# A two-layer hybrid decoder: value blocks side by side, stores on GpSimd's queue, constants and gates at the passage, the last block in three

## The chip, the cores and the metric

The kernel runs on one core of one Trainium2 chip. The metric is the device time of the program in microseconds, the median of several runs. A profile is one execution of the program that the hardware profiler recorded; its times are microseconds from the first instruction's start. The engines are TensorE (PE: matrix products, with its weight loads as PEld), VectorE (DVE), ScalarE (ACT), GpSimd (POOL) and SyncE (SP, which here only issues transfers). Each runs its own queue of instructions in order and waits for the others by semaphores. SBUF is the on-chip memory, PSUM the accumulators that PE writes.

## The reference

The input `x` is 1024 tokens of 1024 features in float32. Two layers with residuals follow, then a final RMS norm. Layer 0 is a gated linear recurrence and layer 1 is forgetting attention, both widened by a SiLU gate:

```python
def fox_mixer(h, w_in, b_f, w_out):            # layer 1, h = rms_norm(x, norm_g[1])
    u = h @ w_in                               # q, k, v, gate: 1024 each; 16 forget logits
    cum = cumsum(log_sigmoid(f_logit + b_f), axis=1)
    logits = q @ k.T / sqrt(64) + cum[query] - cum[key]      # 16 heads of 64
    p = softmax(where(key <= query, logits, -1e30))
    return (p @ v * silu(gate)) @ w_out
...
x = x + lru_mixer(rms_norm(x, norm_g[0]), ...)
x = x + fox_mixer(rms_norm(x, norm_g[1]), ...)
return rms_norm(x, final_g)
```

In layer 0 the mixer is a causal convolution over 4 tokens, two block-diagonal sigmoid gates, a first-order recurrence over the tokens of 1536 channels, and an output product.

## The kernel before, in words

**Products.** PE multiplies float32 numbers as pairs: each operand is split into a rounded high part and the remainder (`to_hi`, line 82, and `to_lo`, line 95), and a product takes three matmuls (high by high, low by high, high by low; lines 121 to 123 for most). Weights come through `split_weights` (line 98): a load into the buffer `wf` by SP, a cast to `wh` by ACT, the remainder `wl` by POOL or DVE. The buffers have rings: three `wf`, four `wh`, four `wl`. All matmuls go through `matmul` and `transpose` (lines 53 and 57), so in the profile they have lines 54 and 58, and one goes by the names of the tiles.

**PSUM.** There are three rings of two tiles: "g" (one bank: projections, products), "S" (two banks: scores, and the transposed probabilities under the name `pt`) and "O" (one bank: weighted values, small things).

**Order.** The code is a trace, and a planner orders each engine's queue after a model of the times. It may put a later instruction forward if an earlier one would wait. An order is forced where the code stands in `tc.issue_after(i)`: the instructions in it that lie on the engine of `i` come behind `i`. `run` (line 783) uses it to lay out the attention by hand: a string says which of three streams takes the next step, "0" the weighing of a head, "1" the scores of the next, "." a filler (projections for later heads, near the end the output product).

**Layer 0** (lines 175 to 462) goes over 12 channel blocks. At its end the passage to layer 1 (lines 437 to 462) adds the last output products to `x`, stores `x` to DRAM (`x1d`), splits it into the operands `hT` of layer 1 and forms its norms (`rms_row`, with the tile `rs` and the row `rsrow`).

**The start of layer 1** (lines 476 to 636). The causal mask and constant rows of the operand tiles `T` (keys) and `U` (queries) are set first, by POOL and DVE. `kq_units` (line 551) projects keys and queries, here the first half of the tokens for the first two heads. `values(0)` (line 502) projects the values of four heads together with the 16 forget logits: eight blocks of 128 tokens, each over eight k of 128 features, tile `vps`, even blocks in "g" and odd ones in "S"; at the end of a block ACT and DVE take it to the split values `v`, and DVE takes the logits to `fz`. `forget` (line 607) transposes four blocks of `fz` (tile `fps`), forms the log-sigmoids and their running sums, and stores them as pairs (`cumd`), from where they are loaded into rows of `T` and `U`. Line 631 calls ten steps of `values(0)`, `forget(0)`, the rest of the values, `forget(1)`; the second token half of `kq_units` follows at line 932.

**Attention**, head by head (line 941). `maxima` (line 655) makes the scores of 128 queries in S, DVE adds the mask and takes the maximum `m`, ACT takes the exponential `p` with its sum. When a head's eight sums are there, they are inverted, transposed (`tr`), copied to `rc`, stored (`recd`, line 697) and loaded again as rows for all 64 features of the head (`recb`, line 701). `scale` (line 707, POOL) multiplies the gate `sg` by these rows; `weigh` (line 712) transposes `p`, splits it and multiplies it by the values into `yo`; `gated` (line 759, POOL) multiplies `yo` by the gate. Up to pair 5 the result is stored (`y1d`) and loaded near the end; pairs 6 and 7 are split in place by `split_y` (line 797), the former at lines 968 and 980. After every fourth head `values(1)` to `values(3)` run without logits (line 974): half the weights are split ahead of the head's last streams, the rest behind, and all blocks lie in "g".

**The output.** `partial` (line 830) multiplies pairs 0 to 5 by the output weights (`wf<-in_wo`), adds the residual that SP loads (`xp<-x1d`, line 838), and stores it back (`x1d<-xp`, line 842). `turned` (line 861) takes blocks of 128 tokens: it transposes the residual, adds the products of pairs 6 and 7 (tile `turn`, halves of 512 features), ACT squares with a sum (line 891), DVE multiplies by the norm's gain (lines 893 and 896). For the second half of the tokens each block ends at once: `root_mean` (line 905), the scaling of both halves (ACT line 897, DVE line 898), two stores.

Of the kernel before, what the change touches and what calls it, by code (L numbers as in the profile page):

```python
# [11 lines left out]
F32 = mybir.dt.float32  # L12
# [5 lines left out]
P = 128  # L18
SEQ = 1024
HALF = 512  # L20
KT = 8
# [17 lines left out]
def trunk(ctx: ExitStack, tc: tile.TileContext, xt, w0, wg, wo0, pc, gn, gf, w1, wv, wf, bf, wo1, out):  # L39
# [431 lines left out]
    with ExitStack() as l1:  # L471
# [16 lines left out]
        for s in range(2):  # L488
            nc.gpsimd.memset(f32(T[s][64:, 1]), 1.0)
# [12 lines left out]
        def values(g):  # L502
# [11 lines left out]
            for st in range(8):  # L514
                if ex and st % 2:
                    pt = ps.tile([P, SEQ], F32, tag="S", name="vps")[:, : 256 + ex]
                else:
                    pt = ps.tile([P, 256 + ex], F32, tag="g", name="vps")
                c = (st % 4) * P
                for k in range(KT):  # L520
                    xh, xl = hT[st // 4][k]
                    wh, wl = parts[k]
                    xh, xl = xh[:, c : c + P], xl[:, c : c + P]
                    matmul(pt, xh, wh, start=k == 0, stop=False)
                    matmul(pt, xl, wh, start=False, stop=False)
                    matmul(pt, xh, wl, start=False, stop=k == KT - 1)
                    if k % 4 == 1:
                        yield
# [22 lines left out]
        def kq_units(pair, parts=((1, (0, 1)), (0, (0, 1)))):  # L551

            for is_k, hs in parts:
# [78 lines left out]
        for _ in range(10):  # L632
            next(first)
        forget(0)
        drain(first)
        forget(1)
# [18 lines left out]
        def maxima(hd, c):  # L655
# [31 lines left out]
            if hd == HEADS - 1 or c == 1:  # L687
# [9 lines left out]
                nc.sync.dma_start(recd[hd, b0:b1], rc[:nb])  # L697
# [3 lines left out]
                nc.sync.dma_start(  # L701
# [128 lines left out]
        def partial(todo):  # L830

            for db, c in todo:
# [28 lines left out]
        def turned(c, q):  # L861
# [11 lines left out]
            for b in range(2):  # L873
                cs = slice(q * 256 + b * P, q * 256 + (b + 1) * P)
                ss = ssq[c][:, 4 * q + 2 * b : 4 * q + 2 * b + 2]
                for h, hs in enumerate(halves):
                    pt = ps.tile([P, HALF], F32, tag="gO"[c * b], name="turn")

                    for i in range(4):
                        x = xs[4 * h + i][:, b * P : (b + 1) * P]  # L880
                        matmul(pt[:, i * P : (i + 1) * P], x, ident, start=i == 0, stop=False, is_transpose=True)
                    for k in range(2):
                        yh, yl = (z[:, cs] for z in y1[c][6 + k])
                        wh, wl = (z[:, k::2] for z in late_w[h])
# [5 lines left out]
                    sq = at.tile([P, HALF], F32, tag="xp", name="sq1", bufs=2)  # L890
                    nc.scalar.activation(sq, pt, AF.Square, accum_out=ss[:, h : h + 1])
                    if c == 0 or h == 0:
                        nc.vector.tensor_tensor(res[b][:, hs], pt, grow[:, hs], ALU.mult)
                        yield
                if c == 1:
                    r = root_mean(ss, lambda: nc.vector.tensor_tensor(res[b][:, hs], pt, grow[:, hs], ALU.mult))
                    nc.scalar.activation(res[b][:, halves[0]], res[b][:, halves[0]], AF.Copy, scale=r)
# [43 lines left out]
        for hd in range(HEADS):  # L941
# [25 lines left out]
            if hd == 14:  # L967
                split_y(1, 6, yos[6, 1])
# [10 lines left out]
            if hd == 13:  # L979
                split_y(0, 6, yos[6, 0])  # L980
# [90 lines left out]
```

## Time and profile before

| | us |
|---|---|
| three runs | 1137.04, 1137.51 (median), 1138.75 |
| the profiled execution, its own time | 1138.24 |
| its span, first to last instruction | 1136.5 |
| PE busy | 1116.5 |
| DVE, ACT, POOL busy | 757.9, 592.1, 163.5 |
| granted PE clock, mean | 0.999 of full |

How to read the lines below: a row of the order of time has the start, the duration, the engine, the line, the operation, output<-inputs, their shapes, the number of instructions that the row merges, and in brackets how long the engine stood idle before and for whom. A matmul's duration overlaps the next one's start, so its pace is read from starts. A row of the waits reads: who <- for whom: total us, times, longest. A row of the chain has start, length, what; it is the chain of work that ended last, followed back. In the page, x is the number of instructions. A row of SPq is SP's queue, with issues of transfers.

### The profile page before, as it was taken

The numbers are of one execution on the slowest core, as the hardware profiler recorded it, in microseconds if no ns is written. First come the engines' busy times: TensorE is split into PE (matmuls) and PEld (weight loads), VectorE is DVE, ScalarE is ACT, GpSimd is POOL, SyncE is SP. The second block draws the span as 40 slices with busy tenths as digits, with TensorE's granted clock in tenths as the row PEclk, the third lists the DMA queues.
The fourth block names the chain that finished last, engine by engine and source line by source line (L and its number), as shares of the span: only waits on it lengthen the run. The fifth ranks groups of instructions, "written<-read, shape, count | busy, mean of one in ns | idle before, by whom it ended". The sixth has DMA issues, their size and how long they took to land.

```text
span 1136.5 us, 15822 instructions
## 1 busy us (share of the span) xinstructions
PE 1116.5 (98%) x5713; PEld 937.5 (82%) x5713; DVE 757.9 (67%) x1276; ACT 592.1 (52%) x1081; POOL 163.5 (14%) x105
## 2 busy tenths in 40 slices
PE   8999999999999999999999999999999999999997
PEld 7787888888888887888888888888888888878886
DVE  7589756876568689666676466764666645676645
ACT  8388345354453666365555355553555534554435
POOL 1212112121121201420010100101001010010110
PEclk9999999999999999999999999999999999999999
DMA  6111121111202114433525215242142431665445
GB/s 215 52 42 51 42 61 38 52 51 42 61 28 61 51 53 147 130 108 95 121 71 117 71 59 123 80 108 79 58 116 78 114 86 47 180 176 164 155 145 185
DMA packets 63702, 105.43 MB, mean 93 GB/s; under 512 B 9508, under 2 KB 24484, under 8 KB 63624
## 3 DMA queue, kind: packets, MB, share of 16 engines
q1 hardware_dynamic: 63624, 104.42, 31.8%
q8 instruction: 45, 0.74, 0.3%
q14 instruction: 33, 0.27, 0.1%
HBM read 63.30 MB, written 15.93 MB: 70 GB/s over the span
## 4 chain that ended last, share of the span: by engine, by line
PE 89%; DVE 3%; ACT 2%; issue 2%; DMA 2%; POOL 1%; SPq 0%; POOLq 0%; ACTq 0%; DVEq 0%
PE gps L54 33%; PE ops L54 15%; PE ups L54 11%; PE vps L54 7%; PE S L54 6%; PE O L54 6%; PE pt L58 5%; PE turn L54 3%; PE gate L54 2%; DVE sq L162 1%; POOL wl L96 1%; DMA x<-in_xt 1%; DVE wl L96 0%; DVE x L453 0%; DMA wf<-in_wo 0%
## 5 line engine op out<-in xcount | busy, mean ns | idle before, releaser
L54 PE MATMUL gps<-hh,wh 128*128 128x512 f32 x576 | 228.9, 398 | 0.0
L54 PE MATMUL gps<-hl,wh 128*128 128x512 f32 x576 | 226.7, 394 | 0.0
L54 PE MATMUL gps<-hh,wl 128*128 128x512 f32 x576 | 226.6, 393 | 0.0
L85 ACT CAST wh<-wf 128x512 fp32r<-128x512 f32 (+2 forms) x156 | 94.3, 607 | 144.2 <-PE gps L54 47.2
L683 ACT ACTIVATE p<-S,m 128x128 f32<-128x128 f32 (+7 forms) x128 | 94.9, 741 | 135.5 <-DVE m L678 134.4
L96 POOL TENSOR_TENSOR wl<-wf,wh 128x512 fp32r<-128x512 f32 (+1 forms) x60 | 98.1, 1639 | 395.9 <-ACT wh L85 342.8
L96 DVE TENSOR_TENSOR pl<-pt,ph 128x512 fp32r<-128x512 f32 (+1 forms) x198 | 98.6, 540 | 81.3 <-ACT ph L85 81.0
L54 PEld LDWEIGHTS gps<-hl,wh 128*128 128x128 f32 x576 | 108.2, 188 | 24.5
L54 PEld LDWEIGHTS gps<-hh,wl 128*128 128x128 f32 x576 | 108.6, 189 | 19.8
L54 PEld LDWEIGHTS gps<-hh,wh 128*128 128x128 f32 x576 | 108.5, 188 | 19.8
L678 DVE CUSTOM_DVE_ANT_0 S<-S,mask 128x128 f32<-128x128 f32 (+7 forms) x128 | 97.3, 760 | 30.5 <-PE S L54 28.9
L710 POOL TENSOR_TENSOR sg<-sg,recb 64x1024 f32<-64x1024 f32 (+1 forms) x17 | 39.2, 2306 | 460.2 <-DMA recb<-recd 444.6
L85 ACT CAST ph<-pt 128x512 fp32r<-128x512 f32 (+1 forms) x198 | 83.6, 473 | 30.6 <-PE pt L58 25.3
L54 PE MATMUL S<-T,U 96*128 96x512 f32 (+7 forms) x384 | 92.2, 349 | 2.0 <-ACT p L683 2.0
L96 DVE TENSOR_TENSOR wl<-wf,wh 128x512 fp32r<-128x512 f32 x96 | 72.1, 756 | 26.0 <-ACT wh L85 25.3
L361 DVE TENSOR_TENSOR x<-x,ops 128x512 f32<-128x512 f32 x80 | 54.0, 681 | 50.6 <-PE ops L54 50.6
L54 PEld LDWEIGHTS S<-T,U 128*128 128x128 f32 (+1 forms) x384 | 68.7, 190 | 15.9 <-ACT p L683 3.2
L54 PE MATMUL ups<-hh,wh 128*128 128x512 f32 x192 | 75.9, 395 | 4.3 <-ACT hh L87 2.4
L58 PE MATMUL pt<-ident,p 128*128 128x128 f32 x576 | 79.3, 273 | 0.0
L58 PEld LDWEIGHTS pt<-ident,p 128*128 128x128 f32 x576 | 67.4, 140 | 12.4 <-issue 2.2
L54 PE MATMUL vps<-wh,hh 128*128 128x256 f32 (+1 forms) x256 | 73.7, 288 | 3.0 <-DVE sg L649 2.1
L54 PE MATMUL ops<-yh,wh 128*128 128x512 f32 x192 | 76.1, 396 | 0.5 <-DVE x L453 0.5
(176 smaller groups left out, 2259.0 us busy)
## 6 DMA issues: line engine op xcount, KB each, us to landing
wf<-in_w SPq DMA_DIRECT2D x100, 256.0 KB
wf<-in_wo SPq DMA_DIRECT2D x64, 128.0 KB
U<-qkh SPq DMA_DIRECT2D x64, 128.0 KB
T<-qkh SPq DMA_DIRECT2D x28, 256.0 KB
x<-in_xt SPq DMA_DIRECT2D x16, 256.0 KB
x1d<-x SPq DMA_DIRECT2D x16, 256.0 KB
wf<-in_wv SPq DMA_DIRECT2D x16, 256.0 KB
U<-qkl SPq DMA_DIRECT2D x32, 128.0 KB
```

Of the source, the lines that this page charges most:

```text
L54: pe[0] = nc.tensor.matmul(*args, **kw)
L58: pe[0] = nc.tensor.transpose(*args)
L85: nc.scalar.copy(hi, src)
L96: return eng.tensor_tensor(lo, src, f32(hi), ALU.subtract)
L162: eng.tensor_tensor(parts[0], parts[0], sq, ALU.add)
L361: nc.vector.tensor_tensor(x, x, pt, ALU.add)
L678: nc.vector.tensor_tensor_reduce(S[:, :n], S[:, :n], mask[:, SEQ - n :], -1.0, -NEG, ALU.add, ALU.min, accum_out=m)
L683: seen[0] = nc.scalar.activation(p, S[:, :n], AF.Exp, bias=m, scale=-1.0, accum_out=sums[:, i : i + 1])
L710: nc.gpsimd.tensor_tensor(sg, sg, recs[hd // 2][rows, cs], ALU.mult)
```

## The change

Six things change.

- **Values.** In the groups without logits, blocks 0 and 1 run side by side: k 0 to 3 of block 0, k 0 to 3 of block 1, k 4 to 7 of block 0, k 4 to 7 of block 1. Odd blocks lie in "S" in all groups.
- **Constants.** The constant rows and the mask are set after the first two steps of `values(0)`, which hold the split of all its weights.
- **Forget gates.** The transposes are ordered behind PE's last traced matmul. `forget(1)` moves behind all values and lies between the second token half's projections: two transposes, two filler steps (twelve matmuls), the third, two more steps, the fourth and the rest. For the first two heads the casts of that half go from DVE to ACT.
- **Queues.** The store of the sums, the load of their rows and the store of the output sums are issued by POOL instead of SP.
- **Splits.** The two `split_y` of pair 6 have their ACT cast ordered behind the last exponential traced.
- **Last block.** The last 128 tokens of all go in parts of 512, 256 and 256 features, the third in a "g" tile; their sums of squares are added in two steps. The last `run` has 20 steps in place of 18.

```diff
-        mask = tu.tile([P, SEQ], BF16, name="mask")
-        nc.gpsimd.memset(mask, 0.0)
-        nc.gpsimd.affine_select(
-            out=mask, in_=mask, pattern=[[-1, SEQ]], compare_op=ALU.is_ge, fill=NEG, base=SEQ - P, channel_multiplier=1
-        )
...
-        for s in range(2):
-            nc.gpsimd.memset(f32(T[s][64:, 1]), 1.0)
-            for u in U[s][s:]:
-                nc.vector.memset(f32(u[64:, 1]), 0.0)
-                nc.vector.memset(f32(u[64:68, 1]), -1.0)
+        def fixed_rows():
+            for s in range(2):
+                nc.gpsimd.memset(f32(T[s][64:, 1]), 1.0)
+                for u in U[s][s:]:
+                    nc.vector.memset(f32(u[64:, 1]), 0.0)
+                    nc.vector.memset(f32(u[64:68, 1]), -1.0)
...
-            for st in range(8):
-                if ex and st % 2:
+            todo = [(st, k) for st in range(8) for k in range(KT)]
+            if not ex:
+                todo[: 2 * KT] = [(st, k) for h in range(2) for st in range(2) for k in range(h * 4, h * 4 + 4)]
+            pts = {}
+            for st, k in todo:
+                if k == 0:
+                    if st % 2:
                         pt = ps.tile([P, SEQ], F32, tag="S", name="vps")[:, : 256 + ex]
                     else:
                         pt = ps.tile([P, 256 + ex], F32, tag="g", name="vps")
+                    pts[st] = pt
+                pt = pts[st]
...
+                if k < KT - 1:
+                    continue
...
-                eng = nc.vector if pair == 0 else nc.scalar
                 def use(h, pt):
+                    eng = nc.scalar if pair or h else nc.vector
...
             for i in range(4):
-                transpose(pt[:HEADS, i * P : (i + 1) * P], fz[:, half * 4 + i], ident)
+                if half and i > 1:
+                    yield
+                with tc.issue_after(pe[0].ins):
+                    transpose(pt[:HEADS, i * P : (i + 1) * P], fz[:, half * 4 + i], ident)
...
         first = values(0)
-        for _ in range(10):
-            next(first)
-        forget(0)
+        next(first)
+        next(first)
+        fixed_rows()
+        mask = tu.tile([P, SEQ], BF16, name="mask")
+        nc.gpsimd.memset(mask, 0.0)
+        nc.gpsimd.affine_select(
+            out=mask, in_=mask, pattern=[[-1, SEQ]], compare_op=ALU.is_ge, fill=NEG, base=SEQ - P, channel_multiplier=1
+        )
+        take(first, 8)
+        drain(forget(0))
         drain(first)
-        forget(1)
...
-                nc.sync.dma_start(recd[hd, b0:b1], rc[:nb])
+                nc.gpsimd.dma_start(recd[hd, b0:b1], rc[:nb])
...
-                nc.sync.dma_start(
+                nc.gpsimd.dma_start(
                     recs[pair][rows, b0 * P : b1 * P],
...
-                nc.sync.dma_start(x1d[c, :, db], x)
+                nc.gpsimd.dma_start(x1d[c, :, db], x)
-        ssq = [const.tile([P, 8], F32, name=f"ssq{c}") for c in range(2)]
+        ssq = [const.tile([P, 8 + c], F32, name=f"ssq{c}") for c in range(2)]
...
-                ss = ssq[c][:, 4 * q + 2 * b : 4 * q + 2 * b + 2]
-                for h, hs in enumerate(halves):
-                    pt = ps.tile([P, HALF], F32, tag="gO"[c * b], name="turn")
+                parts = ((0, 4), (4, 2), (6, 2)) if c * q * b else ((0, 4), (4, 4))
+                ss = ssq[c][:, 4 * q + 2 * b :][:, : len(parts)]
+                for h, (d0, nd) in enumerate(parts):
+                    hs = slice(d0 * P, (d0 + nd) * P)
+                    pt = ps.tile([P, HALF], F32, tag="gO"[c * b] if h < 2 else "g", name="turn")[:, : nd * P]
...
-                    nc.scalar.activation(sq, pt, AF.Square, accum_out=ss[:, h : h + 1])
-                    if c == 0 or h == 0:
+                    nc.scalar.activation(sq, pt, AF.Square, accum_out=ss[:, min(h, ss.shape[1] - 1)].unsqueeze(1))
+                    if c == 0 or h < len(parts) - 1:
                         nc.vector.tensor_tensor(res[b][:, hs], pt, grow[:, hs], ALU.mult)
+                        if h == 1 and c == 1:
+                            nc.vector.tensor_tensor(ss[:, 0:1], ss[:, 0:1], ss[:, 1:2], ALU.add)
+                            ss = ss[:, 0::2]
                         yield
...
-        drain(kq_units(0, ((1, (1,)), (0, (1,)))))
+        fill = kq_units(0, ((1, (1,)), (0, (1,))))
+        gates1 = forget(1)
+        for _ in range(2):
+            next(gates1)
+            take(fill, 2)
+        drain(gates1)
+        drain(fill)
...
-                split_y(1, 6, yos[6, 1])
+                with tc.issue_after(seen[0].ins):
+                    split_y(1, 6, yos[6, 1])
...
-                split_y(0, 6, yos[6, 0])
+                with tc.issue_after(seen[0].ins):
+                    split_y(0, 6, yos[6, 0])
...
-        run("." * 18, fill=chain(turned(1, 0), turned(1, 1)), side=finish())
+        run("." * 20, fill=chain(turned(1, 0), turned(1, 1)), side=finish())
```

More of the change, by code (lines that the diff above doesn't have):

```diff
@@ L513, in values @@
             Vs[2 * g], Vs[2 * g + 1] = [], []
-            for st in range(8):
-                if ex and st % 2:
-                    pt = ps.tile([P, SEQ], F32, tag="S", name="vps")[:, : 256 + ex]
-                else:
-                    pt = ps.tile([P, 256 + ex], F32, tag="g", name="vps")
-                c = (st % 4) * P
[L520 to L528, printed above, removed]
+            todo = [(st, k) for st in range(8) for k in range(KT)]
[5 more added lines that the diff above has]
+                    if st % 2:
+                        pt = ps.tile([P, SEQ], F32, tag="S", name="vps")[:, : 256 + ex]
+                    else:
+                        pt = ps.tile([P, 256 + ex], F32, tag="g", name="vps")
+                    pts[st] = pt
+                pt = pts[st]
+                c = (st % 4) * P
+                xh, xl = hT[st // 4][k]
+                wh, wl = parts[k]
+                xh, xl = xh[:, c : c + P], xl[:, c : c + P]
+                matmul(pt, xh, wh, start=k == 0, stop=False)
+                matmul(pt, xl, wh, start=False, stop=False)
+                matmul(pt, xh, wl, start=False, stop=k == KT - 1)
+                if k % 4 == 1:
+                    yield
+                if k < KT - 1:
+                    continue
                 r_ = rms1[st // 4][:, st % 4 : st % 4 + 1]
@@ L896, in turned @@
                     r = root_mean(ss, lambda: nc.vector.tensor_tensor(res[b][:, hs], pt, grow[:, hs], ALU.mult))
[L897 to L898 removed]
+                    lo, hi = halves
+                    nc.scalar.activation(res[b][:, lo], res[b][:, lo], AF.Copy, scale=r)
+                    nc.vector.tensor_scalar(res[b][:, hi], res[b][:, hi], r, None, ALU.mult)
                     for hs in halves:
```

10 lines of the change are left out of this document (5 added, 5 removed).

## The prediction, made before the change was run

> **What bounds the kernel now.** I read the page first, then who waited for whom with TensorE (PE) alone, then the order of time around each of PE's waits.
>
> ```profile
> span 1136.5 us, 15822 instructions
> ...
> PE 1116.5 (98%) x5713; PEld 937.5 (82%) x5713; DVE 757.9 (67%) x1276; ACT 592.1 (52%) x1081; POOL 163.5 (14%) x105
> ```
>
> PE is busy 1116.5 of 1136.5 us. The change adds no matrix work and removes none, so all it can win is time in which PE stands still, and all it can lose is new standing. PE's waits (us in total, times, longest); the two rows of ups and warm belong to the first layer and to the start, which the diff does not touch:
>
> ```profile
> PE vps L54 <- DVE sg L649: 2.1, 3, 0.7
> PE S L54 <- ACT p L683: 2.0, 2, 1.2
> PE ups L54 <- DVE us L271: 1.9, 1, 1.9
> PE fps L58 <- DVE fz L537: 1.4, 1, 1.4
> PE warm L54 <- DVE epst L67: 1.1, 1, 1.1
> PE vps L54 <- ACT wh L85: 0.9, 3, 0.3
> PE vps L54 <- POOL wl L96: 0.8, 1, 0.8
> PE vps L54 <- DVE wl L96: 0.7, 3, 0.2
> ```
>
> The other six rows make 7.9 us, 0.7% of the span. A wait costs more than its idle time, because the first matmuls after it start at a wider pace; so where I can I count from start to start. About 0.2% (2.3 us) is what a measurement of this kernel can tell from no change.
>
> **Values, the three later groups of heads.** The first of them, PE in order of time:
>
> ```profile
> 638.06 0.28 PE L54 MATMUL O<-pl,v 128*128 128x128 f32 x1
> 638.64 0.39 PE L54 MATMUL vps<-wh,hh 128*128 128x256 f32 x1 [0.30 <-ACT wh L85]
> ...
> 639.71 0.28 PE L54 MATMUL vps<-wh,hl 128*128 128x256 f32 x1
> 639.83 0.28 PE L54 MATMUL vps<-wl,hh 128*128 128x256 f32 x1
> 640.81 0.39 PE L54 MATMUL vps<-wh,hh 128*128 128x256 f32 x1 [0.70 <-DVE sg L649]
> ```
>
> Block 0 has done all but its last six matmuls (638.64 to 639.83, three of them left out here) and waits for the last quarter of the value weights, cast and remainder; then block 1 waits for a PSUM tile "g", which the gate projection's eviction still holds. At the pace of 0.12 us (639.71 to 639.83) the six take 0.72; with as much as 0.06 for the O product, the 2.75 us from 638.06 to 640.81 hold 2.75 - 0.78 = 1.97 us of loss. The table has three such places: 5.9 us in all.
>
> After the change block 1 lies in an "S" tile, and its first four k (12 matmuls, 12 x 0.12 = 1.44 us) come ahead of block 0's second half. From 638.12 they last until 639.56. The remainder that block 0 needs ends before that, at 639.31:
>
> ```profile
> 638.62 0.69 DVE L96 TENSOR_TENSOR wl<-wf,wh 128x512 fp32r<-128x512 f32 x1
> ```
>
> Block 2, the next to ask for a "g" tile, comes only after block 1, long after 640.81. So nothing of the 1.97 need remain. What is late next is the S tile of block 7: the following head's transposes want it, and two casts and two subtractions must empty it first. I charge 0.2 us for that in each group (an estimate, a tenth of the loss): 3 x (1.97 - 0.2) = 5.3. Ends: 3.7 (the idle time alone, 2.1 + 0.9 + 0.7) and 5.9.
>
> **The passage between the layers.** Constants first, POOL's queue, then PE and VectorE (DVE):
>
> ```profile
> 467.89 1.85 POOL L489 MEMSET T<- 64x1024 f32 x2
> 469.81 1.34 POOL L96 TENSOR_TENSOR wl<-wf,wh 128x544 fp32r<-128x544 f32 x1
> ```
>
> ```profile
> 471.21 0.39 PE L54 MATMUL vps<-wl,hh 128*128 128x272 f32 x1 [0.76 <-POOL wl L96]
> ...
> 473.45 1.02 PE L54 MATMUL rsrow<-rs,onesf 128*128 128x512 f32 x2
> ```
>
> ```profile
> 472.38 0.86 DVE L149 TENSOR_SCALAR rs<-ident,rms 128x128 f32<-128x128 f32 x4
> ```
>
> The memsets stand in POOL's queue ahead of the last remainder of the value weights. Moved behind it, they free PE's wait, 0.76 us idle and some 0.1 of pace. But 2.2 us later in PE's order stands rsrow, which needs `rs`, done at 472.38 + 0.86 = 473.24. If PE comes there 0.9 earlier, at 472.55, it waits 0.7 of it again, unless DVE, whose own memsets move too, is also earlier. Ends 0.2 and 0.9; I take 0.5.
>
> The forget gates of the second half:
>
> ```profile
> 491.99 0.48 PE L54 MATMUL gps<-hh,wh 128*128 128x512 f32 x1
> 493.91 0.28 PE L58 MATMUL fps<-ident,fz 128*16 128x128 f32 x1 [1.44 <-DVE fz L537]
> ```
>
> ```profile
> 490.41 1.91 POOL L96 TENSOR_TENSOR wl<-wf,wh 128x512 fp32r<-128x512 f32 x1 [17.80 <-PE vps L54]
> ```
>
> The third transpose waits for block 6's gates and holds up the key projection: 1.92 us from start to start where a projection matmul fills 0.23 (the pace of two, 2 x 0.12 for half the columns), so 1.7 us. Now twelve projection matmuls, 12 x 0.23 = 2.8 us, stand ahead of it, so block 6's gates are there before it asks. What is late next is the second projection matmul's remainder: 490.41 + 1.91 = 492.32, 0.1 after PE asks, and the next quarter's after it, which POOL makes no sooner. I take 1.4 (ends 0.8, half of it eaten by those remainders, and 1.7). The cumulative sums reach the attention's operands while PE is still at the projections that follow; that cover gone, the score products would wait for them. The pair-0 cast that moves from DVE to ScalarE (ACT) in the second half is one for one and hidden in the same place.
>
> **Sums and output sums on POOL's queue; splits behind the exponentials.** PE's two waits on an S tile (2.0 us) lie in heads 13 and 14. At the first, the chain and ACT's order show:
>
> ```profile
> 1015.16 2.95 DVE wl L96
> ```
>
> ```profile
> 1019.29 0.62 ACT L85 CAST yhh<-yo 128x512 fp32r<-128x512 f32 x1 [2.98 <-POOL yo L765]
> 1019.81 0.57 ACT L683 ACTIVATE p<-S,m 128x384 f32<-128x384 f32 x1
> ```
>
> ACT had head 13's split ahead of the exponential that frees the tile. The new order puts that cast behind the exponentials, worth 0.52 us (1019.81 - 1019.29); nobody waits for the cast before the output's last part. The rest of this wait came from DVE's remainder, 2.95 us instead of the 0.69 above, beside POOL's scaling; where such a meeting falls after the change is open. At the second wait the chain goes over the queue of SP:
>
> ```profile
> 1050.13 2.69 DMA recd<-rc
> ...
> 1054.08 3.38 DMA wf<-in_wo
> ```
>
> Now the queue itself. 17 stores of sums, 17 broadcasts and 16 output sums, 50 issues, leave SP. No DMA of this trace is issued by POOL. There a store will wait for DVE's copy, and the broadcast for the store's landing; behind them on POOL stand scaling and gating, which need that broadcast anyway, and an output sum waits for DVE's addition with the same two behind it.
>
> ```profile
> POOL sg L710 <- DMA recb<-recd: 444.6, 16, 44.7
> ...
> ACT wh L85 <- DMA wf<-in_wo: 11.1, 6, 3.2
> ```
>
> ```profile
> SPq L838 <- DMA x1d<-xp: 14.1, 11, 1.9
> ```
>
> POOL stands 444.6 us for the broadcast as it is, so a later one is covered. What is not covered is the last row: SP's next load of output sums waits until the store has landed, and the output weights queue behind that load. If POOL's stores land later by L, the weights do, and ACT, which six times waits for them, holds its exponentials. L is bounded below by -1.3 us (14.1 / 11, the whole wait gone with the sums that stood on SP) and above by 2.7 (a store's whole way a second time, as at 1050.13). I take L = 0: SP loses the sums' 2.69 us in front, POOL's store loses about as much in its own issue. Then the term is the split's 0.5 and half of the other 1.5, less 0.2 for new meetings of POOL and DVE: 1.0 (ends 2.0, and -1.5 where each of the six waits grows by 0.42, a third of the 1.3).
>
> The Trainium skill (DMA: Bandwidth & Descriptors, Specifications) gives about 1 us to the first byte from GpSimd's queue and 0.6 us from SP's, which speaks against the move. By it L would be 0.4, an estimate, and six times that would turn this term from 1.0 to -1.4 and the sum from 8.5 to 6.1; no trace shows the figure so far.
>
> **The last block in three.**
>
> ```profile
> 1130.71 0.60 ACT L891 ACTIVATE sq<-turn 128x512 f32<-128x512 f32 x1 [0.82 <-PE turn L54]
> ```
>
> ```profile
> 1131.50 0.68 DVE L896 TENSOR_TENSOR res<-turn,grow 128x512 f32<-128x512 f32 x1
> 1132.10 0.15 DVE L912 RECIPROCAL ssq<-ssq 128x1 f32<-128x1 f32 x1
> ```
>
> Behind the last matmul the square and the product lie one after the other. At half the columns each takes between half its time and all of it: 0.64 us less at best, nothing at worst. I take 0.3: the end also has one more square and one more addition. Twelve matmuls of 256 columns at 0.12 replace six of 512 at 0.23, nothing for PE.
>
> **Sum.** 5.3 + 0.5 + 1.4 + 1.0 + 0.3 = 8.5 us. The profiled execution took 1138.24 us (span 1136.5 and 1.7 around it), so 1129.7; it was 0.7 above the median of 1137.51, so **1129.0** as a median. All best ends make 5.9 + 0.9 + 1.7 + 2.0 + 0.6 = 11.1 (1126.4), all worst 3.7 + 0.2 + 0.8 - 1.5 + 0 = 3.2 (1134.3).
>
> **Rivals.**
> 1. *The slower store.* In heads 13 to 15 the S waits stay and ACT's six waits for output weights each grow by L: 6 x L against the 7.5 us of the other terms, so from L = 1.3 us the kernel is slower. At L = 2 it is 1137.5 - 7.5 + 12 = 1142. For it: the 14.1 us, 11 times, in SP's row. Against: PE stood only twice in these heads, though ACT waited six times. Chance 0.07.
> 2. *The S tile is taken early.* The planner may put block 1's first half into an idle moment before the head's weighing is done, as nothing orders it behind; then one of two S tiles is gone, and scores and transposes take turns. If that costs in each group what the arrangement wins there, 1.77 us, the values' 5.3 are gone, and if the exponentials' wait for a tile doubles (2.0) little of the rest is left: 1137.5 - 8.5 + 5.3 + 2.0 = 1136.3, no difference. Against: PE's only waits on S are the two above, so the tiles are mostly asked for in time. Chance 0.07.
> 3. *The waits are filled by others.* Values win their idle time alone (3.7), the others nothing, because the next instruction of each queue is as late: 1133.8. For it: rsrow and the second remainder above. Chance 0.14.
>
> **How the numbers follow.** My forecast has 0.72. Faster by over 0.2%: forecast and rival 3, less 0.04 for their ends, 0.82; the same: rival 2 and part of those ends, 0.10; slower: rival 1 and a little of those ends, 0.08. The range runs from just under the best ends, 1126.2, to 1135.0, which takes in the worst ends and rival 3 and leaves out rivals 1 and 2.
>
> **What would show it.** Right: no wait of vps on sg, wh or wl in the later groups; no fps wait on fz; twelve vps matmuls of block 1 between block 0's halves; yhh casts behind p; the last square at 256 columns. Wrong: S waiting for p more than twice, or PE waiting for output weights in heads 13 to 15 (rival 1); vps on S ahead of the head's last transposes, with PE waiting there (rival 2).

## The result, and the profile after

| | before | after |
|---|---|---|
| median of the runs, us | 1137.80 (6 runs, 1136.25 to 1138.75) | 1131.47 (6 runs, 1130.81 to 1133.13) |
| ratio, with its 95% interval | | 0.9948 [0.9935, 0.9961] |
| the profiled execution, its own time, us | 1138.24 | 1131.03 |
| its span, us | 1136.5 | 1129.3 |

The kernel is 0.5% faster, 6.3 us by the medians; the forecast was 8.5 us, to 1129.0, in a range from 1126.2 to 1135.0. The time lies in the range although three of the forecast's five terms went wrong.

The page of after, its span and busy times:

```profile
span 1129.3 us, 15843 instructions
...
PE 1114.8 (99%) x5719; PEld 938.5 (83%) x5719; DVE 752.1 (67%) x1276; ACT 593.0 (53%) x1085; POOL 194.1 (17%) x155
```

PE's waits in after (us in total, times, longest):

```profile
PE S L54 <- ACT p L699: 2.4, 1, 2.4
...
PE gps L54 <- DVE qkl L574: 0.5, 1, 0.5
```

All waits of vps and the one of fps are gone. Two S waits have become one, longer than both together (2.4 us in place of 2.0), and the wait of gps on `qkl` is new.

To see where the time went, both traces were cut at the same matmuls, from start to start. "Sums of head 0" is the row of tr for that head.

| stretch | before, us | after, us | difference | the prediction's term |
|---|---|---|---|---|
| first group of values, first to last matmul | 28.10 | 27.10 | -1.00 | -0.5, constants |
| from there to the first scores | 18.76 | 17.37 | -1.39 | -1.4, forget gates |
| from there to the sums of head 0 | 20.60 | 21.28 | +0.68 | none |
| from there to the sums of head 12, with the three later groups of values | 434.28 | 428.03 | -6.25 | -5.3, values |
| from there to the sums of head 15 | 102.62 | 102.83 | +0.21 | -1.0, queues and splits |
| from there to the last matmul | 62.23 | 62.32 | +0.09 | none |
| from there to the end | 6.25 | 6.85 | +0.60 | -0.3, last block |
| sum | 672.83 | 665.77 | -7.06 | -8.5 |

### The profile page after: what moved, and what is told of

Its sections match the earlier page's. It is cut to its first block, busy times and chain, and to the rows that moved or that the text cites. A ratio compares the mean times of both kernels' runs of the same rounds, so it can differ in the third digit from the quotient of the medians.

```text
span 1129.3 us, 15843 instructions
## 1 busy us (share of the span) xinstructions
PE 1114.8 (99%) x5719; PEld 938.5 (83%) x5719; DVE 752.1 (67%) x1276; ACT 593.0 (53%) x1085; POOL 194.1 (17%) x155
## 4 chain that ended last, share of the span: by engine, by line
PE 92%; DVE 2%; DMA 2%; ACT 2%; issue 1%; SPq 1%; POOL 0%; ACTq 0%; DVEq 0%; POOLq 0%
PE gps L54 33%; PE ops L54 16%; PE ups L54 12%; PE vps L54 8%; PE S L54 6%; PE O L54 6%; PE pt L58 5%; PE gate L54 3%; PE turn L54 3%; DMA wf<-in_wo 1%; PE sscol L54 1%; DMA x<-in_xt 0%; DMA wf<-in_w 0%; ACT yhh L85 0%; DMA yhl<-y1d 0%
## 5 line engine op out<-in xcount | busy, mean ns | idle before, releaser
L54 PEld LDWEIGHTS gps<-hh,wh 128*128 128x128 f32 x576 | 108.6, 189 | 21.3 <-ACT wh L85 1.0
L85 ACT CAST ph<-pt 128x512 fp32r<-128x512 f32 (+1 forms) x198 | 83.6, 473 | 34.5 <-PE pt L58 27.2
L96 DVE TENSOR_TENSOR wl<-wf,wh 128x512 fp32r<-128x512 f32 x96 | 68.5, 718 | 27.9 <-ACT wh L85 27.0
L54 PE MATMUL ups<-hl,wh 128*128 128x512 f32 x192 | 75.8, 395 | 0.0
L54 PE MATMUL ups<-hh,wl 128*128 128x512 f32 x192 | 75.7, 394 | 0.0
```

The lines of the kernel that those rows point to most:

```text
L54: pe[0] = nc.tensor.matmul(*args, **kw)
L85: nc.scalar.copy(hi, src)
L96: return eng.tensor_tensor(lo, src, f32(hi), ALU.subtract)
```

## The experiments

Twelve kernels. In the profiles, the first matmul of layer 0's gates starts anywhere between 58.9 and 61.9 us, in code that no kernel changes. Such a shift may be in any median too (only one execution of each kernel was profiled), and it is why small differences are read below from stretches that begin after it. Each median stands with its ratio to the kernel before, run on the same chip.

**The values, taken apart.** The diffs against the changed kernel, first with the tile and without the written order (A), then with the written order and without the tile (B):

```diff
 A
-            if not ex:
...
-                todo[: 2 * KT] = [(st, k) for h in range(2) for st in range(2) for k in range(h * 4, h * 4 + 4)]
 B
-                    if st % 2:
+                    if ex and st % 2:
                         pt = ps.tile([P, SEQ], F32, tag="S", name="vps")[:, : 256 + ex]
```

A:

> Odd value blocks in S as in the changed kernel, but block 0 whole ahead of block 1 as before. My theory, by the prediction's parting of each group's loss: the tile takes away the wait of block 1 for a g tile (0.7 us idle a group), the side-by-side order the wait of block 0's last six matmuls for the last quarter of the weights (1.0 to 1.2 us a group with its pace). So here about 1.0 us a group comes back: three groups, 3 us, 1134.5. Rival A: the tile is all of it, the second wait having been shadowed by the first; 1131.5 to 1132.0. Rival B: without the tile's help block 1 comes at once and only the remainder's wait is left, but whole: 0.3 to 0.8 us a group, 1132.5 to 1133.5.

B:

> Blocks 0 and 1 side by side, but odd blocks in g as before. My theory: block 1 is now wanted 0.7 us earlier, while its g tile is freed no earlier (by the gate's eviction), so PE waits there ahead of block 1; by then the weights' last quarter is there, so one wait of about 1.5 to 2.0 us a group takes the place of the two: 4.5 to 6 us back, 1136 to 1137.5. Rival A: the order alone wins its half, 1134.5. With the run without the side-by-side order this tells whether the two halves of the edit add up or need each other.

Measured: A 1134.02 us, ratio 0.9958 [0.9946, 0.9970]; B 1138.29 us, ratio 1.0002 [0.9994, 1.0011]. A group of values, first to last matmul, takes 31.24 us before, 29.22 after, 29.22 in A and 31.22 in B (the same within 0.02 in all three groups). So the tile is all of it, and the written order nothing: my theory fell, A's first rival holds. (A's median lies 2.5 us above after's. Its trace is 1.8 longer: 1.4 of that is the late start told of above, and from the first vps to the end it takes 0.36 us more.) The reason is in the order that the planner gave. Before, and in B, PE does 18 matmuls of the group, the first six k of block 0, and the next one waits for the last quarter of the weights. In A it does 18 more without a wait (in the first of the three groups from 637.56 to 640.02). The first seven of them start before the cast of that quarter ends, at 638.38, so they are not the last six of block 0. Once block 1 had a tile of its own, the planner itself put it ahead of the matmuls that would wait; after has the same 18, in the same places among the O products. The trace of A shows it, PE in order of time:

```profile
638.75 0.28 PE L54 MATMUL vps<-wh,hl 128*128 128x256 f32 x1
638.87 0.28 PE L54 MATMUL O<-ph,v 128*128 128x256 f32 x1
638.98 0.27 PE L54 MATMUL vps<-wl,hh 128*128 128x256 f32 x1
```

The O product that stood ahead of the wait before now lies among block 1's matmuls, with no idle time. In B it could not, and the waits of before are back, these two and DVE's remainder, not the one longer wait that my theory had there:

```profile
PE vps L54 <- DVE sg L665: 2.1, 3, 0.7
...
PE vps L54 <- ACT wh L85: 0.9, 3, 0.3
```

**The passage, undone.** Constants at the front and `forget(1)` directly after the values:

```diff
+        fixed_rows()
...
-        fixed_rows()
...
+        drain(forget(1))
...
-        gates1 = forget(1)
-        for _ in range(2):
-            next(gates1)
-            take(fill, 2)
-        drain(gates1)
```

> The constants set at the front and the forget gates of the second half directly behind the values, as before; all else as changed. My theory: by the traces the constants brought 1.0 us up to the last of the first value group and the gates 1.4 up to the first scores, of which 0.5 to 0.7 was lost again to a remainder that came late for the gate projection. So 1.75 us come back, 1133.2. Rival: the values' later groups have slack that takes up what the passage gives, so less than 0.5 us: 1131.5 to 1132.0.

Measured: 1133.04 us, ratio 0.9955 [0.9942, 0.9968]. From the first vps to the sums of head 0 it takes 66.92 us, after 65.75 and before 67.45: 1.17 come back, less than the 1.75 I expected. To the first scores the gates' part gives 18.78 in place of 17.37 (1.41); then 20.43 in place of 21.28, as the wait on `qkl` isn't there. So the gates are worth 0.6 in all.

The constants' part is another matter. POOL and ACT in after, in order of time:

```profile
465.07 0.65 ACT L85 CAST wh<-wf 128x544 fp32r<-128x544 f32 x1 [1.18 <-DMA wf<-in_wf]
465.69 1.83 POOL L484 MEMSET T<- 64x1024 f32 x2 [1.51 <-DMA x1d<-x]
467.59 0.96 POOL L645 MEMSET mask<- 128x1024 bf16 x1
468.50 1.37 POOL L96 TENSOR_TENSOR wl<-wf,wh 128x544 fp32r<-128x544 f32 x1
```

The memsets still stand ahead of the last remainder: the planner has put them forward again, and the edit only changed the places of the two memsets. The remainder starts where they end (468.5), not where its cast ends (465.72). What came sooner is the start of the memsets (466.88 before), which in after wait for a store of `x`, and beside it the cast (466.40 before). Followed back in the order of time, this begins with a meeting of DVE and POOL. Before:

```profile
453.16 0.74 DVE L238 SCALAR_TENSOR_TENSOR hl<-x,gnt,hh 128x512 fp32r<-128x512 f32 x1
453.24 1.81 POOL L96 TENSOR_TENSOR wl<-wf,wh 128x512 fp32r<-128x512 f32 x1 [3.02 <-DVE sq L162]
453.82 1.78 DVE L162 TENSOR_TENSOR sq<-sq 128x512 f32<-128x512 f32 x1
```

After:

```profile
453.06 0.73 DVE L238 SCALAR_TENSOR_TENSOR hl<-x,gnt,hh 128x512 fp32r<-128x512 f32 x1
453.14 3.77 POOL L96 TENSOR_TENSOR wl<-wf,wh 128x512 fp32r<-128x512 f32 x2 [3.01 <-DVE sq L162]
453.73 0.68 DVE L162 TENSOR_TENSOR sq<-sq 128x512 f32<-128x512 f32 x1
```

In both, POOL's remainder starts 0.08 us after DVE's subtraction `hl`, and DVE's addition `sq` 0.58 or 0.59 after the remainder. Before, the remainder ends 1.16 us after the end of `hl`, and the addition 0.55 after the remainder: 1.78 us. After, the addition takes its 0.68, and the remainder (the first of the two, 2.43 us) ends 1.16 after the end of the addition. I read this as a turn: the remainder stands behind `hl`, and then either it or the addition goes next. The next additions to `x`, ACT's casts and the weights' transfers follow 0.9 to 1.2 us sooner where the addition does. It does in 11 of the 14 profiles, and in 3 (before, this run, B) the remainder. B has the constants where after has them, and the instructions of POOL, ACT and DVE up to there in the same order, and still loses the 1.0 us again:

```profile
468.98 0.96 POOL L645 MEMSET mask<- 128x1024 bf16 x1
469.89 1.34 POOL L96 TENSOR_TENSOR wl<-wf,wh 128x544 fp32r<-128x544 f32 x1
...
471.29 0.39 PE L54 MATMUL vps<-wl,hh 128*128 128x272 f32 x1 [0.71 <-POOL wl L96]
```

So the place of the constants is not what won here. What decides whose turn it is stays open.

**The queues.** The three lines back to `nc.sync`, all of them, the two of the sums, or the one of the output sums:

```diff
-                nc.gpsimd.dma_start(recd[hd, b0:b1], rc[:nb])
+                nc.sync.dma_start(recd[hd, b0:b1], rc[:nb])
...
-                nc.gpsimd.dma_start(x1d[c, :, db], x)
+                nc.sync.dma_start(x1d[c, :, db], x)
```

All three on SP:

> The changed kernel with its three kinds of transfer (sums' store, their rows, output sums) back on SP's queue; all else as changed. My theory: the move won nothing. In heads 13 to 15 the changed kernel stands where the kernel before stood (from the last of head 12's sums to those of head 15 it won 0.0 us), its first S wait went with the order of the splits, and its second is longer because a load of output weights landed later and DVE's remainder met POOL's scaling; and its close is longer by about 0.75 us from the last scaling to the end. So back on SP: first S wait still gone, second wait back near 0.8 us in place of 2.4, close back near 3.5 us in place of 4.2: 1.5 to 2.5 us faster than 1131.5, 1129.0 to 1130.0. Rival A, the move removed the first S wait: it comes back and the time is that of the changed kernel or 1 us more, 1131.5 to 1132.5. Rival B, the store on POOL is worth what the prediction's best end gave it (1.5 us): 1133.

The sums on SP:

> Only the sums' store and the load of their rows are back on SP; the output sums stay on POOL. My theory: the close stays long (some queue of POOL is still in use), the second S wait shrinks if it came from POOL standing for the row of sums behind its own output sum; 1130.0 to 1131.5. Rival A (the sums on POOL removed the first S wait): it comes back, 1132 to 1133.

The output sums on SP:

> Only the output sums' store is back on SP; the sums and their rows stay on POOL. My theory: the output weights' late load came from the output sum's way over POOL (its issue of 0.5 us stands behind the scaling, and SP's next load of an output sum waits for it with the weights behind it), so here it lands as early as in the kernel before (3.4 us in the chain in place of 4.7) and the second S wait falls to 1 us or less: 1130.0 to 1131.0. Rival: only the meeting of DVE's remainder with POOL's scaling made the wait; it stays, wherever the meeting stays, and the time is 1131.5.

Measured: all on SP 1129.52 us, ratio 0.9927 [0.9915, 0.9939]; the sums on SP 1129.67, 0.9930 [0.9918, 0.9942]; the output sums on SP 1131.87, 0.9952 [0.9940, 0.9964]. From the first vps to the end the three traces give 663.27, 663.66 and 667.23 us, and that of after 665.77. So the move costs some 2 us, as I thought, but it is the sums' move that costs them; that the output sums' way over POOL made the weights late was wrong (with them on SP again the S wait is 2.6 us, not 1).

**One scaling left out**, to see what the remaining S wait is made of:

```diff
-            scale(hd)
+            if hd != 14:
+                scale(hd)
```

> The changed kernel without POOL's scaling of the gate of head 14, so that head's output lacks the division by its sums; the time alone is read. It tells what the second S wait of the changed kernel is made of. My theory: two causes, a remainder of DVE that lasts 2.07 us in place of 0.42 because it meets this scaling (2.35 us on POOL), and output weights that land late (4.7 us in place of 3.4). Without the scaling the remainder takes 0.4 to 0.5 us and the wait falls from 2.35 to about 0.7, so 1.6 us faster by the trace, 1129.4. Rival A, the late weights alone: the wait stays over 2 us. Rival B, the meeting alone: no wait left.

Measured, one execution: from the sums of head 14 to those of head 15 it takes 19.11 us in place of 20.85, 1.74 less, and the S wait is 0.6. So the meeting makes 1.7 of the wait, the larger part. That the 0.6 that stays comes from late weights is read from the chain and was not tried by itself. After, around that wait:

```profile
1044.03 0.54 POOL L717 DMA_DIRECT2D recb<-recd  x1 [2.21 <-DMA recd<-rc]
1048.93 2.35 POOL L726 TENSOR_TENSOR sg<-sg,recb 64x1024 f32<-64x1024 f32 x1 [1.54 <-DMA recb<-recd]
...
1049.06 0.41 ACT L85 CAST wh<-wf 128x256 fp32r<-128x256 f32 x1 [2.97 <-DMA wf<-in_wo]
1049.50 2.07 DVE L96 TENSOR_TENSOR wl<-wf,wh 128x256 fp32r<-128x256 f32 x1 [1.78 <-ACT wh L85]
1051.49 0.55 DVE L694 CUSTOM_DVE_ANT_0 S<-S,mask 128x384 f32<-128x384 f32 x1
1052.13 0.58 ACT L699 ACTIVATE p<-S,m 128x384 f32<-128x384 f32 x1 [2.67 <-DVE m L694]
```

The same with all on SP:

```profile
1043.43 0.47 SPq L717 DMA_DIRECT2D recb<-recd  x1
1046.99 2.40 POOL L726 TENSOR_TENSOR sg<-sg,recb 64x1024 f32<-64x1024 f32 x1 [23.88 <-DMA recb<-recd]
...
1048.00 0.41 ACT L85 CAST wh<-wf 128x256 fp32r<-128x256 f32 x1 [1.55 <-DMA wf<-in_wo]
1048.44 1.23 DVE L96 TENSOR_TENSOR wl<-wf,wh 128x256 fp32r<-128x256 f32 x1 [0.33 <-ACT wh L85]
1049.60 0.55 DVE L694 CUSTOM_DVE_ANT_0 S<-S,mask 128x384 f32<-128x384 f32 x1
```

Read it from below. The maximum that the exponential needs stands in DVE's queue behind the remainder, the remainder behind the cast, the cast behind the weights. On SP the rows of sums (`recb`) go first and the weights after them: the rows are there 3.56 us after their issue (1046.99 - 1043.43), the weights 3.27 us after theirs (1048.00 - 1044.73), and the scaling is half done when the remainder comes. On POOL the two run at once: the rows take 4.90 us (1048.93 - 1044.03), and by the chain the weights 4.66. Scaling and remainder then begin 0.57 us apart, and the remainder lasts 2.07 us, where it takes 0.43 in the run without the scaling.

The packets in the traces show the two transfers meet. With all on SP the 64 packets of the rows start from 1044.68 to 1045.77 and last 0.19 us each; the 128 of the weights start from 1046.56 to 1047.53 and last 0.05. In after the rows' start from 1045.51 to 1047.61 and last 0.26, and the weights' lie among them, from 1045.99 to 1048.02, and last 0.07. That POOL's transfer starts later explains little: from the issue to the first packet of the rows it is 1.48 us from POOL and 1.25 from SP. This agrees with the Trainium skill (DMA: Bandwidth & Descriptors, Issuing engines are not separate DMA queues): transfers of all issuing engines end up on the same 16 DMA engines and interleave there. A second queue gave no second way, it took away the order of the two.

**The splits.** Without their place behind the exponentials, with the changed kernel's queues, and then with all on SP:

```diff
-                with tc.issue_after(seen[0].ins):
-                    split_y(1, 6, yos[6, 1])
+                split_y(1, 6, yos[6, 1])
```

> The two splits of pair 6 without their place behind the exponentials; all else as changed. My theory: the order of the split took away the first S wait, or its 0.52 us of it. So that wait is back with 0.5 to 1.4 us, and the time is 1132.0 to 1132.9 where nothing later takes it up. Rival A (the transfers' queue took that wait away): no change, 1131.5, and the exponentials of heads 13 and 14 wait for S no longer than in the changed kernel.

> All three kinds of transfer on SP and the two splits of pair 6 without their place behind the exponentials. The first run with all on SP kept 0.7 us of the first S wait (head 13) where the kernel before had 1.2; with the transfers on POOL that wait was gone whether the splits were ordered or not. My theory: with the transfers on SP the order of the splits is worth the 0.5 us of the prediction; so the S wait of head 13 is 1.2 us again and the end comes 0.5 us later than in the first run, which had 1129.5. Rival: the order is worth nothing here either, and the 0.5 us came from the earlier arrival of head 13 in some other way; the wait stays at 0.7 us.

Measured: 1133.68 us, ratio 0.9963 [0.9950, 0.9976], and 1131.93, 0.9940 [0.9927, 0.9952]. From the sums of head 12 to those of head 15, in us, by kernel (the one without a scaling left out):

| | splits ordered | splits free |
|---|---|---|
| sums on SP | 100.44, 100.73, 101.00, 101.42, 101.53 | 101.79, and 102.62 (before) |
| sums on POOL | 102.42, 102.83 (after), 102.88, 103.47, 104.66 | 102.56 |

On POOL the order of the splits is worth nothing there, and its rival holds: left free, the planner puts head 13's cast behind the exponential by itself (1014.61 after 1011.69). The median's 2.2 above after's is not explained by the splits: that trace starts 2.4 us late, and from the first vps to the end takes 0.27 more. On SP it is worth 0.3 to 2.2, the means 1.2; one of the two traces there is that of before, which differs in more than the splits. With splits free on SP, ACT in head 13:

```profile
1010.89 0.62 ACT L85 CAST yhh<-yo 128x512 fp32r<-128x512 f32 x1 [3.30 <-POOL yo L781]
1011.41 0.57 ACT L699 ACTIVATE p<-S,m 128x384 f32<-128x384 f32 x1
...
1012.13 0.74 PE L54 MATMUL S<-T,U 128*128 128x512 f32 x2 [1.56 <-ACT p L699]
```

ACT waits 3.30 us for POOL's product with an exponential behind that it could have done (its maximum is there at 1008.41). That is more than the 0.52 of the prediction, which counted only the cast. Where the splits are ordered, the table's two rows do not overlap: the sums on POOL cost 2.2 us between their means (101.0 and 103.3).

Taken apart by heads, from sums to sums, the two changes act in different places. From head 13 to head 14 it takes 39.57 us before and 38.0 in all seven kernels with the sums on POOL, the one with free splits among them; on SP it takes 39.83 with free splits, and with ordered ones 38.95, 38.71 and three times 38.0. From head 14 to head 15 it takes 18.4 to 19.5 in the seven kernels with the sums on SP, and 20.5 to 22.6 in the six on POOL that keep the scaling, with ordered or free splits (means 18.9 and 21.3). So either change can take the first S wait away by itself (the move by one trace), and the sums' move costs 2.4 us at the second.

Part of the spread within a row is another meeting, in head 13. After:

```profile
1007.27 0.69 DVE L96 TENSOR_TENSOR wl<-wf,wh 128x512 fp32r<-128x512 f32 x1 [0.52 <-ACT wh L85]
...
1007.47 2.75 POOL L726 TENSOR_TENSOR sg<-sg,recb 64x1024 f32<-64x1024 f32 x1 [2.95 <-DMA recb<-recd]
```

All on SP:

```profile
1006.73 2.40 POOL L726 TENSOR_TENSOR sg<-sg,recb 64x1024 f32<-64x1024 f32 x1 [40.09 <-DMA recb<-recd]
1006.78 2.89 DVE L96 TENSOR_TENSOR wl<-wf,wh 128x512 fp32r<-128x512 f32 x1 [0.52 <-ACT wh L85]
```

The remainder starts 0.2 us ahead of the scaling in the one and 0.05 behind it in the other, and that is 2.2 us of DVE's time; PE's wait for S there is 0.7 us in the one with all on SP and none in after.

**The last block.** All on SP, with the addition forced ahead of the product, with two parts, and, on top of the first, with the two casts of the first heads on DVE again:

```diff
-            nc.vector.tensor_tensor(r, r, ss[:, :, 1], ALU.add)
-            between()
+            total = nc.vector.tensor_tensor(r, r, ss[:, :, 1], ALU.add)
+            with tc.issue_after(total.ins):
+                between()
...
-                parts = ((0, 4), (4, 2), (6, 2)) if c * q * b else ((0, 4), (4, 4))
+                parts = ((0, 4), (4, 4))
...
-                    eng = nc.scalar if pair or h else nc.vector
+                    eng = nc.scalar if pair else nc.vector
```

> All three kinds of transfer on SP, and in the last block the addition of the sums of squares forced ahead of the product by the gain in DVE's queue. My theory: the product of 256 columns (0.42 us, behind which the addition stood for 0.35) no longer stands between the last square and the root, so the last scaling ends 0.35 us sooner after the last matmul (2.0 us in place of 2.4), and the end comes 0.35 us sooner than in the first run with all on SP. Rival: the root only changes places with the product, as the scaling needs both, and nothing is won.

> All three kinds of transfer on SP, and the last block in two halves as before. My theory: three parts with the addition behind the product won 0.03 us (2.37 us from the last matmul's end to the scaling's end, in place of 2.40), so two parts cost nothing: the end within 0.1 us of the first run with all on SP, by the marks of the trace. Rival: the third part's matmuls of half the width and the extra square cost or win on PE's side, 0.2 us or more either way.

> As the kernel with the addition ahead of the product, and the two casts of the first heads' second token half back on DVE. My theory: the wait of the gate projection on a g tile that DVE's remainder holds, 0.5 us at 508 us and new in the changed kernel, came from the forget gates' move (PE is earlier there), not from the casts; so it stays or grows by the cast's 0.3 to 0.5 us. Rival: ACT's cast stands behind the exponentials of the gates and is what made the remainder late; then the wait goes, 0.5 us faster than the kernel beside it.

Measured: 1129.19 us, ratio 0.9922 [0.9910, 0.9935]; 1129.99, 0.9934 [0.9920, 0.9947]; 1130.00, 0.9928 [0.9915, 0.9940]. From the last matmul's end to the end of ACT's scaling it takes 2.41 us before, 2.38 after and in the other kernels with three parts, 2.40 with two parts, and 2.04 and 2.05 with the addition ahead. So the three parts alone win nothing, and 0.34 with the order. After, behind the last matmul:

```profile
1122.80 0.38 ACT L910 ACTIVATE sq<-turn 128x256 f32<-128x256 f32 x1 [0.46 <-PE turn L54]
...
1123.30 0.42 DVE L918 TENSOR_TENSOR res<-turn,grow 128x256 f32<-128x256 f32 x1 [0.22 <-ACT sq L910]
1123.64 0.15 DVE L932 TENSOR_TENSOR ssq<-ssq 128x1 f32<-128x1 f32 x1
1123.83 0.29 ACT L934 ACTIVATE ssq<-ssq,epst 128x1 f32<-128x1 f32 x1 [0.56 <-DVE ssq L932]
```

With the addition ahead:

```profile
1120.42 0.16 DVE L932 TENSOR_TENSOR ssq<-ssq 128x1 f32<-128x1 f32 x1 [0.22 <-ACT sq L910]
1120.49 0.42 DVE L918 TENSOR_TENSOR res<-turn,grow 128x256 f32<-128x256 f32 x1
1120.61 0.29 ACT L935 ACTIVATE ssq<-ssq,epst 128x1 f32<-128x1 f32 x1 [0.23 <-DVE ssq L932]
```

The planner had put the shorter product ahead of the addition, where the longer one of before stood behind it; the root waited for both. The casts were not the cause of the new wait on `qkl`: with them on DVE it is still 0.6 us, and with the gates back directly after the values it is gone. In the changed kernel DVE does the split of the gates' running sums (`cp`) ahead of the remainder that holds the g tile:

```profile
507.82 0.67 DVE L96 TENSOR_TENSOR cp<-cum,cp 16x512 fp32r<-16x512 f32 x1
508.43 0.67 DVE L574 SCALAR_TENSOR_TENSOR qkl<-gps,qkh 128x512 fp32r<-128x512 f32 x1
```

The kernel with all on SP and the addition ahead has the lowest median of the twelve; its interval overlaps those of the other kernels with the sums on SP, and lies just at the edge of the changed kernel's.

## Why the prediction was right, and where it was not

**Values: right, 5.3 forecast, 6.05 in the groups (3 x 2.02).** The loss of 1.97 that it read from start to start went whole; the 0.2 a group for a late S tile was not needed. Which half of the edit does it was not asked: the planner writes the order itself, and the twelve matmuls written between block 0's halves won nothing.

**Forget gates: the gain was right, 1.4 forecast and 1.39 measured, the loss behind it was not.** It named the weights' remainders as late next. Late next was a g tile held by DVE, 0.55 us of wait and 0.7 with its pace, so half of it went again; the 0.7 that is left lies just below the lower end of 0.8.

**Constants: 0.5 forecast, 1.0 measured, and the step failed.** "Moved behind it, they free PE's wait" did not happen: the memsets were not moved behind it. The prediction had no rival in which this edit does not do what it says. The gain was a meeting of DVE and POOL that fell out otherwise, and that is luck: it falls out as before in 3 of the 14 profiles, two of them of changed kernels. How often it does in the executions that were not profiled is not known.

**Queues and splits: 1.0 forecast, a loss of 0.2 measured.** The step that failed is "I take L = 0", and before it the choice of what to price. SP's wait for the stored output sums did grow, to

```profile
SPq L854 <- DMA x1d<-xp: 34.5, 11, 7.9
```

that is by 1.9 us each on average (34.5 less 14.1, by 11), within the bounds that were set for L; the longest is 7.9. The prediction's estimate of 0.4 us between the two queues' first bytes is 0.23 us (1.48 less 1.25) in the one pair of transfers compared above. But ACT's waits for output weights did not become six times that: they are 9.4 us in 4 in place of 11.1 in 6, and with the output sums alone on POOL the kernel is as fast as with all on SP. What cost was the other pair of transfers: "a later one is covered", said of the broadcast, held for POOL, which waited anyhow, but not for DVE, which the later scaling then met, nor for the weights that share the DMA engines. From head 14 to head 15 that made 19.29 us into 20.85. From head 13 to head 14 the first S wait went, 39.57 us into 38.00, more than the 0.5 that the splits were given; either change can do that by itself. The two cancel, and 0.2 is lost ahead of them.

**Last block: 0.3 forecast, 0.03 measured up to the scaling, as DVE's order took it; and 0.75 lost behind it.** From the end of the last scaling to the end of the span it takes 4.2 us in each of the six kernels with all three kinds of transfer on POOL, 3.64 with the sums alone there, 3.51 with the output sums alone, and 3.43 to 3.45 in the six with none. After, SP's queue at the end:

```profile
1124.87 1.07 SPq L923 DMA_DIRECT2D out_t<-res  x2
```

With all on SP:

```profile
1122.99 0.81 SPq L923 DMA_DIRECT2D out_t<-res  x2
```

The last two issues take 0.26 longer, and the rest lies behind the last store. No step of the prediction had the close in it. Why it is longer was not tried.

**The sum** came out by offsets: 8.5, plus 0.95 for the values' stretch and 0.5 for the constants', less 0.7 behind the gates, 1.3 for heads 12 on and 0.9 for the end, is 7.05, for the 7.06 measured. Of the rivals, the first had its wait and not its consequence; the second was not seen, as no vps or S wait stands where it put one; the third described the gates and the last block. The values' stretch gave 6.25 of the 7.06. The other four terms, 3.2 together in the forecast, gave 0.8, and the 1.0 of the constants in it is luck. So it is the values, with a range that reaches down to 2.5 us of gain, that make the prediction right.

## What to carry to other kernels

Give a stream a resource of its own, here a PSUM tile, before writing its order out: here the planner filled the time by itself, and without the tile the order did nothing. Ask of each moved instruction where it lies in the compiled queue of its engine, since an edit of the source may not move it. And before transfers go to another queue, ask which of two transfers has to land first: here they kept their order on one queue, and from two they shared the DMA engines and both were late.

## What the runs showed of the hardware that was not expected

- Where a remainder of weights on DVE (128x512 or 128x256) and POOL's scaling overlap, the one that starts first goes first, and the other ends later by its wait. In the 14 traces there are 109 such pairs. In 71 the remainder starts later, by 0.01 to 2.39 us, and ends 0.55 to 0.68 us (128x512) or 0.28 to 0.29 us (128x256) after the scaling, so that it takes up to 2.94 us in place of 0.69. In 38 it starts earlier, by 0.03 to 0.68 us, and takes its 0.68 to 0.69, and the scaling up to 2.91 in place of 2.4. This agrees with the Trainium skill (SBUF — State Buffer, SBUF: two separate sides), which has an exclusive lock for the whole instruction, won by the one that starts first.
- The meeting at 453 us fits that too, if one counts the instruction ahead: DVE's `hl` starts 0.08 us before POOL's remainder. Whether the remainder or DVE's next instruction goes when `hl` ends came out one way in 11 profiles and the other way in 3.
- A DMA issue takes POOL 0.52 to 0.73 us of its own time.
- Transfers issued by POOL in this kernel make its end longer, by 0.1 us with 16 of them, 0.2 with 34 and 0.75 with 50.
